# Two more ff tiles computed the plain way ahead of the pairs that use sums of blocks

## The chip, the cores and the metric

The kernel runs on one core of a Trainium2 chip. Five engines of the core work side by side, each through its own list of instructions in a fixed order: PE (matrix products), DVE and ACT (elementwise work), POOL (little here) and SP (issues the loads and stores). An instruction that needs another engine's result waits for it, and all that stands behind it in the same list waits too. The metric is the device time of one execution in microseconds (us).

## What is computed

Two layers of an encoder for T = 576 tokens of width 1024 (512 tokens of new streams and 64 of running ones). Each layer is a SwGLU block, a mixer with three groups of heads, and a second SwGLU block, every one between norms:

```python
D_MODEL = 1024; D_FF = 2816; DEPTH = 2

def _swiglu(x, w_gate, w_up, w_down):
    return (jax.nn.silu(x @ w_gate) * (x @ w_up)) @ w_down

# layer l
x = x + 0.5 * post1(swiglu_1(pre1(x)))
x = x + post2(mixer(pre2(x)))
x = x + 0.5 * post3(swiglu_2(pre3(x)))
```

So there are four SwGLU stages in a run. In each, gate and up are products of a 1024 x 2816 matrix with the 576 tokens.

## The kernel before

**Tiling.** The tokens lie along the free dimension, in two halves of 288 columns (`HALF`). The 1024 rows of x are 8 k tiles of 128, the 2816 columns of a weight are 22 ff tiles of 128. Every product is made of three matmuls (`three`, through `mul`, L68), since each operand is split into a high part and a rest: high x high, high x low, low x high. The names are `wh`, `wl` for a weight, `hh`, `hl` for x, `th`, `tl` for sums of blocks of x. A split is one copy on ACT (L126 or L138) and one subtraction on DVE (L127 or L139).

**The plain way.** `unit` takes one 128-column chunk of a weight, and for 8 k tiles and 2 halves issues 8 x 2 x 3 = 48 matmuls of 288 columns into two PSUM tiles named `u`. Gate and up of one ff tile need two chunks. `evac` then reads them half by half: DVE `g = u * rbc` (L339, gate times the norm's factor), ACT silu (L340), DVE `g = g * u` (L341, times up).

**The way with sums of blocks.** `seven` computes gate and up of two neighbouring ff tiles f and f+1 in one go: the weight is cut into 2 x 2 blocks (k tiles 0 to 3 and 4 to 7, ff tiles f and f+1), the tokens into two halves, and seven block products replace eight, at the price of sums: of weight blocks (DVE L478, L480, L488, L497, 128x1024 each) and of blocks of x (`combine`). Each product is 24 matmuls, a pair 7 x 24 = 168. In the plain way the same two ff tiles take four chunks, 4 x 48 = 192. The products of a pair stand in the order X (x block as it is), Q (t1), X (t2), Q (x block), X (t3), R (x block), X (t4). Q with t1 needs the first sum of x blocks in both of its k groups; R needs the sums of weights' splits that come last.

**A stage** (`ffn`, L327). (1) ff tiles 0 and 1 were loaded ahead as four chunks; `units` computes them for the first half of the tokens, then for the second, as x becomes ready behind the norm. (2) `combine` makes t1 to t4 for two k groups: for each, 8 scaled copies of x blocks on ACT (L427, `b<-x,colg`), four sums on DVE (L436, L438, L440, L442), and four splits into `th` (ACT L138, L141) and `tl` (DVE L139, L142). It ends with the stores of x to DRAM. (3) `evac` of the second half of ff tiles 0 and 1. (4) `for f in range(2, NF, 2)`: ten pairs in `seven`. (5) the down projection.

**Order and buffers.** The order on each engine is set when the program is built, by a list scheduler that takes the code's order and the tiles' dependencies. Raw weights have 6 buffers (`wr`, also the weight sums `ws`), their split parts 7 each (`wh`, `wl`), and matmul results 6 PSUM banks (`mm`), handed out in turn: the seventh `u`, `X`, `Q` or `R` tile can only be begun when the reader of the first is done.

Of the kernel before, what the change touches and what calls it, by code (L numbers as in the profile page):

```python
# [15 lines left out]
P = 128  # L16
# [8 lines left out]
NF = D_FF // P  # L25
# [24 lines left out]
class Net:  # L50
# [276 lines left out]
    def ffn(self, l, j, gpost, gpre, gain, nxt, packed):  # L327
        nc = self.nc
        wg, wu, wd = self.i["ffn_w_gate"][l, j], self.i["ffn_w_up"][l, j], self.i["ffn_w_down"][l, j]
        r, r2, rbc = self.rn, self.rn2, self.rbc  # L330
        g = {}


        def evac(f, hf, pg, pu):
            c0, n = HALF[hf]
            if hf == 0:
                g[f] = self.slot("g")
            t = g[f][:, c0:c0 + n]
            nc.vector.tensor_tensor(t, pg[:, :n], rbc[:, c0:c0 + n], op=ALU.mult)  # L339
            nc.scalar.activation(t, t, AF.Silu)  # L340
            nc.vector.tensor_tensor(t, t, pu[:, :n], op=ALU.mult)  # L341

        chs, self.ahead = self.ahead, None
        for hf in (0, 1):
            o = self.units(chs, hf, 2 if gpost is self.g0 else 4)
            if hf == 0:
                self.until(lambda: 0 in self.stats_done)
                for f in (0, 1):
                    evac(f, 0, o[2 * f][0], o[2 * f + 1][0])
        chs = None  # L350
        ops = self.combine(gain)
        self.until(lambda: 1 in self.stats_done)
        for f in (0, 1):
            evac(f, 1, o[2 * f][1], o[2 * f + 1][1])
        o = None
        for f in range(2, NF, 2):
            self.seven(f, wg, wu, ops, g, rbc)
        ops.clear()
        self.h = {}

        d = []
        for a, (g0, g1) in enumerate(GROUPS):
            first, last = a == 0, a == len(GROUPS) - 1
            gh, gl = {}, {}
            for f in range(g0, g1):
                gh[f], gl[f] = self.slot("gh", F32R), self.slot("gl", F32R)
                self.split(gh[f], gl[f], g.pop(f))
            if last:
                acc = self.slot("acc2")
                self.recall()  # L370
                if gpre is None:
                    self.spawn(self.rows_of_x(), 25.0)

            def run(m, ch, hfs):
                ps = {hf: self.mm("d") for hf in hfs}
                for f in range(g0, g1):
                    for hf in hfs:
                        c0, n = HALF[hf]
                        self.three(ps[hf][:, :n], ch[0][:, f - g0], ch[1][:, f - g0],
                                   gh[f][:, c0:c0 + n], gl[f][:, c0:c0 + n], f == g0, f == g1 - 1)  # L380
                    self.tick()
                for hf in hfs:
                    c0, n = HALF[hf]
                    sl = slice(c0, c0 + n)
                    if first:
                        if hf == 0:
                            d.append(self.slot("d"))
                        nc.scalar.activation(d[m][:, sl], ps[hf][:, :n], AF.Copy)
                        continue
                    nc.vector.tensor_tensor(d[m][:, sl], d[m][:, sl], ps[hf][:, :n], op=ALU.add)  # L390
                    if last:
                        self.square_sum(acc, d[m], sl, m)
                        if gpre is None:
                            nc.scalar.activation(d[m][:, sl], d[m][:, sl], AF.Copy, scale=gpost[m])

            tail = KT - 3 if last else KT
            for m in range(tail):
                run(m, self.cols(wd, m * P, P, g0, g1 - g0), (0, 1))
            if last:
                chs = [self.cols(wd, m * P, P, g0, g1 - g0) for m in range(tail, KT)]  # L400
                self.ahead = [self.cols(*q) for q in nxt]
                for hf in (0, 1):
                    for m in range(tail, KT):
                        run(m, chs[m - tail], [hf])
                    self.after(hf, d, acc, gpost, gpre, (r, r2), packed)
# [1051 lines left out]
```

## Time and profile before

| what | value |
|---|---|
| device time, median of 3 runs (lowest, highest) | 2313.14 us (2313.03, 2313.42) |
| the profiled execution's own time | 2313.43 us |
| span of its trace, first to last instruction | 2311.6 us |
| mean granted clock of PE | 0.979 of 2.4 GHz |
| busy PE, DVE, ACT, POOL | 96%, 69%, 48%, 10% |
| share of the chain that ended last: PE, DVE, ACT | 76%, 14%, 4% |
| the first pair of `seven` in the four SwGLU stages | 30.16, 33.20, 31.21, 33.12 us |
| a later pair | 22.40 us |

The page's first part gives busy time by engine. Windows of the trace give busy time and the granted clock of a stretch. "Idle before" is time in which an engine stood still just before an instruction, and behind it stands what ended that. PE's matmuls overlap, so their pace is read from one start to the next and not from one's length. A pair is counted here from the first start of its product X to the first start of the next pair's.

### The profile page before, as it was taken

Reading aid. Unit: us, or ns where it says so; the run is one execution under the profiler, and the core shown is the slowest. Engines: PE = TensorE matmul, PEld = TensorE weight load, DVE = VectorE, ACT = ScalarE, POOL = GpSimd, SP = SyncE. Lnnn points to the kernel's source line nnn. Section 1 sums busy time; section 2 is a strip of 40 time slices with the busy share of each in tenths; the row PEclk is TensorE's granted clock in tenths of the full one; section 3 lists DMA queues with packets and bytes.
Section 4 is the critical chain, followed back from the end, with each engine's and each line's share of the span. In section 5 each row is a group of like instructions: output and inputs, shape, how many; then the busy total and the mean of one; then the engine's idle time right before and its main releaser. Section 6 shows DMA issues by size and latency. Waiting matters only on the chain.

```text
span 2311.6 us, 39493 instructions
## 1 busy us (share of the span) xinstructions
PE 2217.3 (96%) x15892; PEld 2155.0 (93%) x15892; DVE 1594.7 (69%) x2671; ACT 1114.0 (48%) x1945; POOL 225.4 (10%) x230
## 2 busy tenths in 40 slices
PE   8999999998899899999989999999988998999998
PEld 7999999888799799999979999998887998999998
DVE  6888643787567888744588885438875678877443
ACT  7444442465554644443355444325646546444423
POOL 0000000343301100000020000004332020000000
PEclk9999999999999899999999999999999999999999
DMA  6333442222122233344123334423121312333421
GB/s 195 103 101 92 119 133 83 92 57 77 60 59 65 90 101 96 88 128 132 47 86 101 93 90 122 132 74 101 39 86 48 96 60 83 93 92 103 118 77 42
DMA packets 339787, 211.06 MB, mean 91 GB/s; under 512 B 17634, under 2 KB 319956, under 8 KB 339604
## 3 DMA queue, kind: packets, MB, share of 16 engines
q1 hardware_dynamic: 339604, 208.54, 30.3%
q8 instruction: 125, 2.05, 0.4%
q14 instruction: 58, 0.48, 0.1%
HBM read 190.11 MB, written 18.38 MB: 90 GB/s over the span
## 4 chain that ended last, share of the span: by engine, by line
PE 76%; DVE 14%; ACT 4%; issue 3%; POOL 3%; DMA 0%; SPq 0%; POOLq 0%; DVEq 0%; ACTq 0%
PE d L68 23%; PE X L68 22%; PE Q L68 11%; PE R L68 6%; PE wo L68 4%; PE u L68 3%; DVE zb L706 2%; PE n L68 2%; DVE hl L142 2%; DVE x L256 1%; PE sc L68 1%; DVE d L253 1%; DVE wl L127 1%; DVE wl L139 1%; PE q L68 1%
## 5 line engine op out<-in xcount | busy, mean ns | idle before, releaser
L68 PE MATMUL d<-gh,wh 128*128 128x288 f32 x1408 | 413.5, 297 | 2.7 <-ACT gh L138 2.7
L68 PE MATMUL d<-gl,wh 128*128 128x288 f32 x1408 | 413.9, 295 | 0.0
L68 PE MATMUL d<-gh,wl 128*128 128x288 f32 x1408 | 412.7, 294 | 0.0
L127 DVE TENSOR_TENSOR wl<-wr,wh 128x1024 fp32r<-128x1024 f32 (+2 forms) x174 | 203.4, 1173 | 175.9 <-ACT wh L126 175.1
L126 ACT ACTIVATE wh<-wr 128x1024 fp32r<-128x1024 f32 (+2 forms) x174 | 174.8, 1008 | 287.3 <-PE d L68 163.9
L68 PE MATMUL X<-th,wh 128*128 128x288 f32 x960 | 286.8, 299 | 0.0
L68 PE MATMUL X<-tl,wh 128*128 128x288 f32 x960 | 285.5, 297 | 0.0
L68 PE MATMUL X<-th,wl 128*128 128x288 f32 x960 | 284.5, 296 | 0.0
L68 PEld LDWEIGHTS d<-gh,wh 128*128 128x128 f32 x1408 | 262.3, 187 | 3.6 <-ACT gh L138 3.6
L68 PEld LDWEIGHTS d<-gh,wl 128*128 128x128 f32 x1408 | 264.8, 188 | 0.0
L68 PEld LDWEIGHTS d<-gl,wh 128*128 128x128 f32 x1408 | 264.1, 188 | 0.0
L138 ACT ACTIVATE wh<-wr 128x1024 fp32r<-128x1024 f32 x160 | 168.4, 1055 | 148.0 <-PE R L68 68.5
L139 DVE TENSOR_TENSOR wl<-ws,wh 128x1024 fp32r<-128x1024 f32 x120 | 147.0, 1225 | 105.4 <-ACT wh L138 105.2
L139 DVE TENSOR_TENSOR wl<-wr,wh 128x1024 fp32r<-128x1024 f32 x160 | 194.7, 1222 | 8.2 <-ACT wh L138 6.8
L138 ACT ACTIVATE wh<-ws 128x1024 fp32r<-128x1024 f32 x120 | 127.3, 1060 | 150.4 <-DVE ws L497 97.8
L151 POOL TENSOR_TENSOR p<-m,mhalf 128x3 f32<-128x3 f32 (+1 forms) x14 | 14.4, 1028 | 1739.4 <-DVE m L234 1535.1
L68 PEld LDWEIGHTS X<-th,wl 128*128 128x128 f32 x960 | 183.1, 191 | 0.0
L68 PEld LDWEIGHTS X<-tl,wh 128*128 128x128 f32 x960 | 182.8, 190 | 0.0
L68 PEld LDWEIGHTS X<-th,wh 128*128 128x128 f32 x960 | 182.6, 190 | 0.0
L390 DVE TENSOR_TENSOR d<-d,d 128x288 f32<-128x288 f32 x128 | 55.2, 454 | 179.6 <-PE d L68 179.5
L68 PE MATMUL u<-hh,wh 128*128 128x288 f32 x480 | 148.3, 312 | 3.0 <-ACT x L1363 1.5
L68 PE MATMUL u<-hl,wh 128*128 128x288 f32 x480 | 148.0, 309 | 1.2 <-DVE hl L142 1.2
(364 smaller groups left out, 5857.6 us busy)
## 6 DMA issues: line engine op xcount, KB each, us to landing
wr<-ffn_w_gate SPq DMA_DIRECT2D x160, 256.0 KB, 3.0
wr<-ffn_w_up SPq DMA_DIRECT2D x160, 256.0 KB, 3.4
wr<-ffn_w_down SPq DMA_DIRECT2D x64, 512.0 KB, 4.2
wr<-w_in SPq DMA_DIRECT2D x30, 512.0 KB, 3.7
xd<-x SPq DMA_DIRECT2D x48, 288.0 KB, 2.1
x<-xd SPq DMA_DIRECT2D x48, 288.0 KB, 6.0
wr<-ffn_w_down SPq DMA_DIRECT2D x32, 384.0 KB, 3.6
wr<-w_out SPq DMA_DIRECT2D x16, 512.0 KB, 3.4
```

What stands on the lines that cost most here:

```text
L68: self.nc.tensor.matmul(out, lhsT, rhs, start=start, stop=stop, skip_group_check=onto)
L126: nc.scalar.activation(hi[:, :a * b], raw[:, :a * b], AF.Copy)
L127: nc.vector.tensor_tensor(lo[:, :a * b], raw[:, :a * b], hi[:, :a * b].bitcast(F32), op=ALU.subtract)
L138: nc.scalar.activation(hi, src, AF.Copy)
L139: nc.vector.tensor_tensor(lo, src, hi.bitcast(F32), op=ALU.subtract)
L142: nc.vector.scalar_tensor_tensor(lo, src, scale, hi.bitcast(F32), op0=ALU.mult, op1=ALU.subtract)
L151: self.nc.gpsimd.tensor_tensor(out, m, self.mhalf[:, :n], op=ALU.pow)
L253: nc.vector.scalar_tensor_tensor(d[s][:, sl], d[s][:, sl], gpost[s], bc, op0=ALU.mult, op1=ALU.mult)
L256: nc.vector.tensor_tensor(self.x[k][:, sl], self.x[k][:, sl], d[k][:, sl], op=ALU.add)
L390: nc.vector.tensor_tensor(d[m][:, sl], d[m][:, sl], ps[hf][:, :n], op=ALU.add)
L706: nc.vector.tensor_tensor(zo, qv[rs, :, h:], ev[rs, :, h:], op=ALU.mult)
```

## The change

ff tiles 2 and 3 are taken out of the loop over pairs. Their gate and up chunks go through `cols` and `unit`, as four plain chunks of 48 matmuls in the order gate 2, up 2, gate 3, up 3; behind each up stands `evac` for both halves. The loop over pairs begins at f = 4, so there are nine pairs in a stage in place of ten. `combine` stays where it was, ahead of both.

```diff
         for f in (0, 1):
             evac(f, 1, o[2 * f][1], o[2 * f + 1][1])
         o = None
-        for f in range(2, NF, 2):
+        for f in (2, 3):
+            pg = self.unit(self.cols(wg, f * P))
+            pu = self.unit(self.cols(wu, f * P))
+            for hf in (0, 1):
+                evac(f, hf, pg[hf], pu[hf])
+        for f in range(4, NF, 2):
             self.seven(f, wg, wu, ops, g, rbc)
```

The order on the engines in the second of the four stages (layer 0, second SwGLU). In all stages PE's order differs in this place alone, but for some matmuls of ff tiles 0 and 1 that change places in the first stage.

PE, where ff tiles 0 and 1 end. Before; `bc` is the norm's factor spread over the partitions:

```order
L68 MATMUL u_8304<-hl_8277,wh_7820 128x288
L68 MATMUL u_8304<-hh_8276,wl_7821 128x288
L73 MATMUL bc_8481<-ident_c,rn_7928 128x128 x3
L68 MATMUL X_8515<-hh_7977,wh_8501 128x288
L68 MATMUL X_8515<-hl_7978,wh_8501 128x288
L68 MATMUL X_8515<-hh_7977,wl_8502 128x288
L68 MATMUL X_8515<-hh_7977,wh_8501 128x288
```

PE in the same place now:

```order
L68 MATMUL u_8298<-hl_8271,wh_7814 128x288
L68 MATMUL u_8298<-hh_8270,wl_7815 128x288
L73 MATMUL bc_8475<-ident_c,rn_7922 128x128 x3
L68 MATMUL u_8492<-hh_7971,wh_8488 128x288
L68 MATMUL u_8492<-hl_7972,wh_8488 128x288
L68 MATMUL u_8492<-hh_7971,wl_8489 128x288
L68 MATMUL u_8493<-hh_8152,wh_8488 128x288
```

The 168 matmuls of the first pair (X, Q, X, Q, X, R, X) are gone from here, and 192 plain ones stand in their place; `u_8492` and `u_8493` are the two halves of gate 2.

DVE, where `combine` ends (its last `tl`). Before, with the weight splits of the first pair among its rows:

```order
L440 TENSOR_TENSOR b_8450<-b_8450,b_8444 128x576
L442 TENSOR_TENSOR b_8447<-b_8441,b_8447 128x576
L139 TENSOR_TENSOR wl_8611<-wr_8495,wh_8610 128x1024
L139 TENSOR_TENSOR tl_8465<-b_8450,th_8464 128x576
L139 TENSOR_TENSOR wl_8642<-wr_8512,wh_8641 128x1024
L139 TENSOR_TENSOR tl_8470<-b_8447,th_8469 128x576
L139 TENSOR_TENSOR wl_8674<-wr_8498,wh_8673 128x1024
```

DVE in the same place now (the lines behind L357 have moved by 5, so L440 reads L445 here):

```order
L445 TENSOR_TENSOR b_8444<-b_8444,b_8438 128x576
L447 TENSOR_TENSOR b_8441<-b_8435,b_8441 128x576
L502 TENSOR_TENSOR ws_8737<-ws_8737,wr_8744 128x1024
L139 TENSOR_TENSOR tl_8459<-b_8444,th_8458 128x576
L139 TENSOR_TENSOR tl_8464<-b_8441,th_8463 128x576
L339 TENSOR_TENSOR g_8598<-u_8492,rbc_7921 128x288
L339 TENSOR_TENSOR g_8598<-u_8493,rbc_7921 128x288
```

The two reads of gate 2's banks (L339) stand behind the whole of `combine` and behind three weight sums of the first pair that is left (f = 4).

ACT, behind the norm's factor of the first half (`rbc`). Before:

```order
L215 ACTIVATE rbc_7927<-bc_8288 128x288
L427 ACTIVATE b_8409<-x_7696,colg 128x288
L340 ACT_TABLE_LOAD
L340 ACTIVATE g_8293<-g_8293 128x288
L340 ACTIVATE g_8297<-g_8297 128x288
L427 ACTIVATE b_8409<-x_7697,colg 128x288
```

ACT in the same place now:

```order
L215 ACTIVATE rbc_7921<-bc_8282 128x288
L126 ACTIVATE wh_8663<-wr_8661 128x1024
L340 ACT_TABLE_LOAD
L340 ACTIVATE g_8287<-g_8287 128x288
L340 ACTIVATE g_8291<-g_8291 128x288
L432 ACTIVATE b_8403<-x_7690,colg 128x288
```

The split of up 3's weight (`wh_8663`) has come in ahead of the table load, the silu and the copies for `combine`. It takes the eighth `wh` where there are seven buffers, and so waits for PE to be done with the first chunk of ff tile 0.

## Rows read from the trace of the kernel before

**Rows 1.** The page: busy time, and the chain that ended last.

```profile
PE 2217.3 (96%) x15892; PEld 2155.0 (93%) x15892; DVE 1594.7 (69%) x2671; ACT 1114.0 (48%) x1945; POOL 225.4 (10%) x230
PE 76%; DVE 14%; ACT 4%; issue 3%; POOL 3%; DMA 0%; SPq 0%; POOLq 0%; DVEq 0%; ACTq 0%
```

**Rows 2.** Windows: the four first pairs, then a later one.

```profile
core 0: us, PE busy (x) PEld busy (x) DVE busy (x) ACT busy (x) POOL busy (x), PEclk, DMA share, GB/s
46.75:76.91 30.16, 24.71 (x171) 23.78 (x169) 28.07 (x36) 19.82 (x32) 0.00 (x0) 0.94 0.30 86
773.77:806.97 33.20, 26.69 (x172) 25.29 (x169) 31.46 (x41) 21.53 (x35) 0.00 (x0) 0.85 0.28 80
1188.86:1220.07 31.21, 25.05 (x172) 24.12 (x170) 28.50 (x37) 20.55 (x34) 0.00 (x0) 0.95 0.29 85
1917.42:1950.54 33.12, 26.61 (x172) 25.33 (x170) 31.46 (x41) 21.54 (x35) 0.00 (x0) 0.90 0.28 79
76.91:99.31 22.40, 22.40 (x171) 22.40 (x169) 19.83 (x26) 10.79 (x15) 0.00 (x0) 1.00 0.34 97
```

**Rows 3.** PE's waits over the run: total us, times, longest us.

```profile
PE R L68 <- DVE wl L139: 12.8, 4, 3.5
PE Q L68 <- ACT th L138: 7.1, 4, 2.6
PE R L68 <- ACT wh L138: 3.3, 4, 1.4
PE Q L68 <- DVE tl L139: 1.4, 4, 0.4
```

**Rows 4.** Chain in the second stage's first pair: start, us, what.

```profile
778.65 0.37 DVE g L339
...
787.94 0.67 DVE tl L139
788.61 1.15 DVE wl L139
...
789.80 0.61 PE R L68
```

**Rows 5.** Windows, columns as in rows 2: two inside first pairs, one ahead.

```profile
783.20:793.44 10.24, 6.82 (x28) 6.12 (x27) 10.24 (x12) 6.67 (x12) 0.00 (x0) 0.50 0.37 108
59.57:62.98 3.41, 2.91 (x12) 2.92 (x13) 3.41 (x5) 0.41 (x2) 0.00 (x0) 0.50 0.50 142
1179.20:1182.50 3.30, 3.30 (x16) 3.30 (x16) 2.85 (x6) 2.89 (x7) 1.77 (x1) 0.50 0.07 18
```

**Rows 6.** PE's timeline: plain matmuls of the third stage, then a first pair.

```profile
1183.18 0.29 PE L68 MATMUL u<-hl,wh 128*128 128x288 f32 x1
...
1188.49 0.29 PE L68 MATMUL u<-hh,wl 128*128 128x288 f32 x1
...
790.20 0.44 PE L68 MATMUL X<-th,wh 128*128 128x288 f32 x1
790.44 0.44 PE L68 MATMUL X<-tl,wh 128*128 128x288 f32 x1
```

**Rows 7.** DVE's timeline, second stage: two evacuations, and the end of `combine`.

```profile
774.49 0.46 DVE L339 TENSOR_TENSOR g<-u,rbc 128x288 f32<-128x288 f32 x1 [3.34 <-ACT rbc L215]
...
782.54 0.45 DVE L341 TENSOR_TENSOR g<-g,u 128x288 f32<-128x288 f32 x1
...
789.65 0.76 DVE L139 TENSOR_TENSOR tl<-b,th 128x576 fp32r<-128x576 f32 x1
```

**Rows 8.** ACT's timeline, second stage, around the table load.

```profile
762.74 1.28 ACT L340 ACT_TABLE_LOAD   x1
...
764.72 3.08 ACT L427 ACTIVATE b<-x,colg 128x288 f32<-128x288 f32 x7
...
774.05 0.41 ACT L215 ACTIVATE rbc<-bc 128x288 f32<-128x288 f32 x1 [3.53 <-PE bc L73]
```

**Rows 9.** DMA issues on SP, loads of 512 KB: median us to landing.

```profile
wr<-ffn_w_down SPq DMA_DIRECT2D x64, 512.0 KB, 4.2
```

## The prediction

> **What bounds the kernel now.** I read the page first: PE is busy 96% of the span and holds 76% of the chain that ended last, DVE 14% [rows 1]. So a change pays if it takes matmuls away, or if it takes away time in which PE stands or runs at a lower clock. This one adds matmuls, and so the question is what it takes from PE's idle time. I then looked at windows by stage. A pair of `seven` takes 22.40 us at full clock, with PE busy throughout [rows 2]: 168 matmuls, 0.1333 us each. But the first pair of each of the four SwGLU stages takes 30.16, 33.20, 31.21 and 33.12 us, at a granted clock of 0.94, 0.85, 0.95 and 0.90 [rows 2]. Together that is 127.69 us where four later pairs take 89.60: an excess of 38.1 us.
>
> PE's waits say what most of it is. R waits 12.8 us for `wl` and 3.3 for `wh`, Q waits 7.1 us for `th` and 1.4 for `tl`, each four times in the run [rows 3]; these sixteen waits lie in the four first pairs, one of each kind in each, and come to 24.6 us. What they wait for is shown by the chain: in the second stage's first pair it runs through DVE, in the rest of `combine` and the weight splits that stand between its rows, up to PE's R at 789.80 us [rows 4]. Here DVE is the engine that sets the end: 31.46 us busy of 33.20 [rows 2]. The other 38.1 - 24.6 = 13.5 us is clock: inside the first pairs there are stretches with a granted clock of 0.50 (1.2 of 2.4 GHz), behind the waits: 10.24 us long in the second stage, 3.41 in the first [rows 5]. There matmuls start 0.24 us apart [rows 6] in place of 0.133.
>
> **What the change removes.** The first pair, with its waits and its lower clock: -127.69 us. Of the pair's work beside PE, four weight sums on DVE, and seven weight splits on ACT and DVE with it, are gone from the place where DVE sets the end.
>
> **What it adds on PE.** 4 chunks of 8 x 2 x 3 = 48 plain matmuls, 192 a stage. Their pace is on the trace: 41 plain matmuls in the third stage start between 1183.18 and 1188.49 us, 40 steps of 0.1328 us [rows 6], the pair's pace within reading. I take the pair's 0.1333: 192 x 0.1333 = 25.6 us a stage, 102.4 us in four. So with PE never waiting: 102.4 - 127.69 = **-25.3 us**. Against a pair without waits a stage pays 3.2 us for its 24 more matmuls (24 x 0.1333), so the change pays if over 3.2 of a stage's 9.5 us of excess go.
>
> The Trainium skill, TensorE: Matmul & The Clock Gate, section Back-to-back issue gap, gives N / 2.4 + 2.5 ns for a warm matmul by itself, 122.5 ns at 288 columns; the trace's 133 ns disagrees, and decides. By the page's figure four stages would come to an estimated 94.1 us and the change to -33.6; the sum above doesn't use it.
>
> **Do the waits go, or move?** The plain chunks need x and their weights only, not `combine`. PE begins gate 2 where X began (T = 773.77 us in the second stage [rows 2]), and the first pair that is left begins 25.6 us later, at 799.4. The last of `combine` ended at 789.65 + 0.76 = 790.4 us before [rows 7], 9 us ahead of that. What can still hold PE is its banks: six in turn, two to a chunk. Each release against its need in the second stage:
> - up 2 (T + 6.4 = 780.2 us) takes the banks of ff tile 0's second half, last read ahead of ff tile 1's L339, which stood at 778.65 [rows 4].
> - gate 3 (T + 12.8 = 786.6) takes those of ff tile 1's second half, last read by L341 at 782.54 + 0.45 = 783.0 [rows 7]: 3.6 us to spare, and less by what `combine` comes later (below).
> - up 3 (T + 19.2 = 793.0) takes gate 2's own, read by two L339 that stand behind all of `combine`. This is the tightest place, and it hangs on ACT.
>
> **ACT and DVE, second and fourth stage.** The split of up 3's weight now stands ahead of the table load, the silu and the copies for `combine`. It waits for a `wh` buffer until ff tile 0's first chunk is done; 48 of the plain matmuls come after that, so about 773.7 - 6.4 = 767.3 us. Behind it: its own 1 us (as a long row, 1.1), the load 1.28, two silu, eight copies (seven take 3.08 [rows 8], so 3.5): they end near 773.4, where they ended at 764.72 + 3.08 = 767.8. Of these 5.6 us DVE stood idle for 3.34 anyway, waiting for the second half's `rbc` [rows 7, 8]. From 773.4 on DVE has, by the order, 6 long rows (1024 columns), 16 of 576 and 4 of 288 ahead of the first L339 of gate 2. From start to start these take 1.14, 0.67 and 0.37 us [rows 4]: 6.84 + 10.72 + 1.48 = 19.0 us. So that L339 starts at 792.4 and ends at 792.9 us, level with the 793.0 at which it is needed. I take a wait of nought here, and keep 1 us a stage for the range: the count leaves no room. In the first and third stage no split stands ahead of the copies, and L339 is there some us early.
>
> **SP.** Four loads of 512 KB take the place of eight of 256 KB, with the same bytes. One of 512 KB lands 4.2 us from its issue [rows 9], and the chunks are needed 6.4 us apart. Nothing, hidden behind the chunk before; without that cover 4.2 us for one chunk.
>
> **Sum.** The profiled execution took 2313.43 us, of which the trace spans 2311.6, and the rest stays. 2313.43 - 25.3 = 2288.1; the median lies 0.3 us below it: **2288.0 us** forecast, 1.1% less.
>
> **Rivals.**
> *The clock stays low* (0.06). The 13.5 us might not hang on these waits. For it: the clock is 0.50 in other stretches as well, in 1179.20 to 1182.50 us with PE busy throughout [rows 5]. Against: inside later pairs it is 1.00 [rows 2], and the four first pairs differ only by their waits. It gives 2288.0 + 13.5 = 2301.5. The Trainium skill, TensorE: Matmul & The Clock Gate, section "A second HAM failure mode: psum-queue depth-cycling", has a form of it: short idle times between groups of matmuls, from banks that are turned over, make the clock go up and down. Rows 5 agree that the clock falls behind short waits; that bank turnover alone makes such waits here, no run shows.
>
> *ACT's delay gets through* (0.09). If DVE loses 3 us more in the two stages with the moved split, as by standing still once more for `th` the way it did for `rbc` (3.34 us [rows 7]), up 3 waits 3 us there, and a stretch of 3.41 us at half clock may follow [rows 5], worth 1.7: 2 x 4.7 = 9.4, so 2297.4. For it: the count above has no room; against: in that count ACT has its `th` ready while DVE is in a long row.
>
> *PE waits for DVE as long as now* (0.04), the other sign. The queue on DVE, not the place of the pair, would set the end: it is the bound, 31.46 of 33.20 us [rows 2], and the change takes nothing from `combine`. If up 3 must wait for it as Q and R do, 24.6 us of waits and 13.5 of clock stay, and the 96 more matmuls (12.8 us) come on top: 2313.1 + 12.8 = 2325.9. It decides from the point at which a stage loses (25.3 + 4.6) / 4 = 7.5 us in waits and clock, with the first L339 some 6 us behind T + 19.2. Against: 25.6 us of PE work lie now between the start of the queue and its end, where the first wait was 6.4 us behind X.
>
> That the change does not what it says: the order of the changed program shows the 192 matmuls where they should be, so under 0.01.
>
> **How the numbers follow.** Forecast 0.80, its own range 2285.5 to 2293: downwards the plain pace of 0.1328 (0.4 us) and one stretch at half clock less elsewhere (1.7 us), upwards 1 us of waiting and half of such a stretch in each of two stages, and 1 us for the rest. The first two rivals lie above it. To hold 8 in 10 the range goes up into ACT's delay: 2285.5 to 2297.5. What a measurement can tell here from no change is about 0.2%, 4.6 us. Faster by more: forecast and the first two rivals, with a little taken off, 0.94; within 0.2%: 0.02; slower by more: 0.04.
>
> **What would show it.** In the profile after: no PE waits of Q and R for `th`, `tl`, `wh`, `wl` in rows like 3; the time from the last of ff tile 1 to the first X 25.6 us in each stage, at a granted clock of 1.00; the first pair left 22.40 us. Wrong would be: `u` waiting for DVE L339 over 1 us in a stage, an X later than T + 26, or the clock at 0.50 within it.

## The result, and the profile after

The changed kernel took 2285.9 us (median; 2283.0 to 2288.3) against 2313.1 us before: a ratio of 0.9884, 95% interval 0.9867 to 0.9901, so 27.2 us or 1.2% faster. The forecast was 2288.0. The profiled execution took 2284.6 us, with a span of 2282.8.

The windows of the trace after, from each stage's T (where the first plain chunk begins) to the first X, and two pairs behind it. Columns: window, its length, busy time of PE, PEld, DVE, ACT, POOL, granted clock, DMA share, GB/s.

```profile
46.61:72.18 25.57, 25.57 (x194) 25.57 (x194) 23.40 (x31) 12.91 (x22) 0.00 (x0) 1.00 0.30 86
764.85:790.43 25.58, 25.58 (x196) 25.58 (x194) 25.09 (x35) 16.59 (x29) 0.00 (x0) 1.00 0.18 52
1170.55:1196.12 25.57, 25.57 (x195) 25.57 (x193) 23.93 (x33) 15.28 (x28) 0.00 (x0) 1.00 0.29 83
1896.24:1921.81 25.57, 25.57 (x195) 25.57 (x194) 23.21 (x33) 15.30 (x27) 0.00 (x0) 1.00 0.22 63
72.18:94.58 22.40, 22.40 (x171) 22.40 (x169) 15.69 (x21) 10.21 (x14) 0.00 (x0) 1.00 0.25 73
790.43:812.82 22.39, 22.39 (x171) 22.39 (x169) 15.55 (x21) 10.17 (x14) 0.00 (x0) 1.00 0.29 84
```

These stand where the first four lines of [rows 2] stood. The 30.16, 33.20, 31.21 and 33.12 us have become 25.57 or 25.58 in every stage, PE is busy from end to end, and the clock is 1.00. The first pair that is left takes 22.40 us like any other. In the second stage DVE is busy 25.09 us of 25.58: the work that held PE is still there, beside PE now.

The chain that ended last, second stage (start, us, what), shows the same; where DVE stood in [rows 4] there is only PE:

```profile
764.77 0.33 PE bc L73 x3
765.10 25.49 PE u L68 x192
790.59 3.19 PE X L68 x24
```

None of the four kinds of waits of [rows 3] is left in PE's waits over the run; what PE's rows of `u` still wait for (waiter, line, what for: total us, times, longest) lies outside the four stretches above, and Q, R and X have no row:

```profile
PE u L68 <- ACT x L1368: 1.5, 2, 0.9
PE u L68 <- DVE on L839: 1.4, 2, 0.7
PE u L68 <- DVE hl L142: 1.2, 4, 0.4
```

The place that the prediction called the tightest, in DVE's and ACT's timelines of the second stage (start, us, engine, line, operation):

```profile
758.03 1.06 ACT L126 ACTIVATE wh<-wr 128x1024 fp32r<-128x1024 f32 x1 [3.11 <-PE u L68]
759.11 1.28 ACT L340 ACT_TABLE_LOAD   x1
761.09 3.51 ACT L432 ACTIVATE b<-x,colg 128x288 f32<-128x288 f32 x8
...
762.93 0.76 DVE L441 TENSOR_TENSOR b<-b,b 128x576 f32<-128x576 f32 x1
763.60 1.22 DVE L485 TENSOR_TENSOR wr<-wr,wr 128x1024 f32<-128x1024 f32 x1
765.21 0.76 DVE L139 TENSOR_TENSOR tl<-b,th 128x576 fp32r<-128x576 f32 x1 [0.39 <-ACT th L138]
...
781.16 1.43 DVE L139 TENSOR_TENSOR tl<-b,th 128x576 fp32r<-128x576 f32 x2
782.50 0.83 DVE L339 TENSOR_TENSOR g<-u,rbc 128x288 f32<-128x288 f32 x2
```

The split of up 3's weight waits 3.11 us for PE and starts 6.8 us ahead of T = 764.85 (6.4 were counted); the copies end at 764.6, 0.25 ahead of T (0.4). The first L339 of gate 2 starts at T + 17.65 and is done about T + 18.1; up 3 needs it at T + 19.2. So there were 1.1 us of room where the prediction counted 0.1. In the first, third and fourth stage it starts at T + 13.4, 16.6 and 16.6, with 5.4, 2.1 and 2.2 us of room.

### The profile page after: what moved, and what is told of

It reads as the page before. It is cut to its first block, busy times and chain, and to the rows that moved or that the text cites. A ratio compares the mean times of both kernels' runs of the same rounds, so it can differ in the third digit from the quotient of the medians.

```text
span 2282.8 us, 39582 instructions
## 1 busy us (share of the span) xinstructions
PE 2214.3 (97%) x15988; PEld 2157.1 (94%) x15988; DVE 1554.9 (68%) x2627; ACT 1093.4 (48%) x1917; POOL 225.6 (10%) x230
## 4 chain that ended last, share of the span: by engine, by line
PE 80%; DVE 10%; ACT 3%; issue 3%; POOL 3%; DMA 0%; SPq 0%; POOLq 0%; DVEq 0%; ACTq 0%
PE d L68 24%; PE X L68 20%; PE Q L68 10%; PE u L68 8%; PE R L68 5%; PE wo L68 4%; DVE zb L711 2%; PE n L68 2%; PE sc L68 1%; DVE x L256 1%; DVE hl L142 1%; DVE d L253 1%; DVE wl L127 1%; PE q L68 1%; PE oT L68 1%
## 5 line engine op out<-in xcount | busy, mean ns | idle before, releaser
L127 DVE TENSOR_TENSOR wl<-wr,wh 128x1024 fp32r<-128x1024 f32 (+3 forms) x190 | 224.0, 1183 | 177.7 <-ACT wh L126 176.2
L126 ACT ACTIVATE wh<-wr 128x1024 fp32r<-128x1024 f32 (+3 forms) x190 | 191.5, 1011 | 297.2 <-PE d L68 166.9
L68 PE MATMUL X<-th,wh 128*128 128x288 f32 x864 | 255.7, 296 | 0.0
L68 PE MATMUL X<-tl,wh 128*128 128x288 f32 x864 | 254.9, 295 | 0.0
L68 PE MATMUL X<-th,wl 128*128 128x288 f32 x864 | 254.0, 294 | 0.0
L68 PE MATMUL u<-hh,wh 128*128 128x288 f32 x736 | 223.4, 305 | 3.1 <-ACT x L1368 1.5
L68 PE MATMUL u<-hl,wh 128*128 128x288 f32 x736 | 223.0, 303 | 1.2 <-DVE hl L142 1.2
L68 PE MATMUL u<-hh,wl 128*128 128x288 f32 x736 | 221.7, 302 | 0.0
L68 PEld LDWEIGHTS X<-th,wl 128*128 128x128 f32 x864 | 162.8, 188 | 0.0
L68 PEld LDWEIGHTS X<-tl,wh 128*128 128x128 f32 x864 | 162.2, 188 | 0.0
```

Source lines behind the costliest of these rows:

```text
L68: self.nc.tensor.matmul(out, lhsT, rhs, start=start, stop=stop, skip_group_check=onto)
L126: nc.scalar.activation(hi[:, :a * b], raw[:, :a * b], AF.Copy)
L127: nc.vector.tensor_tensor(lo[:, :a * b], raw[:, :a * b], hi[:, :a * b].bitcast(F32), op=ALU.subtract)
```

## Experiments

**What did Q and R wait for?** The kernel before with all ten pairs, and the work of `combine` left out:

```diff
         for q in range(2):
-            b = []
-            for kp in (q, q + 2):
-                for hf in range(2):
...
-            nc.vector.tensor_tensor(b21, b11, b21, op=ALU.subtract)
-            part("t4", b21)
+            ops["t1"].append(self.h[q, 0])
+            ops["t2"].append(self.h[q, 1])
+            ops["t3"].append(self.h[q + 2, 0])
+            ops["t4"].append(self.h[q + 2, 1])
```

> The kernel before, all ten pairs in seven, but t1 to t4 are given x blocks as they are: the copies, sums and splits of combine are left out, so gate and up come out as other numbers. Theory (Q and R of the first pair wait because combine stands in DVE's and ACT's queues around the pair's own sums and splits): all sixteen waits go, 24.6 us, and the 13.5 us of low clock with them; the first pairs take 22.4 us each, 2313.1 - 38.1 = 2275.0 us. Rival (the pair's own weight sums and splits are what R waits for, 16.1 us of the waits): Q's 8.5 us go, R's stay with most of the clock: 2300 to 2305 us.

Measured 2274.1 us, ratio 0.9837 (0.9823 to 0.9852). All four first pairs take 22.40 us; those of the second and third stage:

```profile
763.96:786.36 22.40, 22.40 (x171) 22.40 (x169) 19.40 (x26) 12.44 (x19) 0.00 (x0) 1.00 0.40 118
1167.17:1189.57 22.40, 22.40 (x171) 22.40 (x170) 20.64 (x27) 12.71 (x20) 0.00 (x0) 1.00 0.40 118
```

No wait and no low clock is left in them, R's included, although all weight sums and splits of the pair are still made. So `combine` was the cause of all sixteen waits, of R's through the queue: the weights' rows stood between and behind its rows. It also gives the floor for ten pairs, 2274: the changed kernel lies 12 us above it, about the price of its 96 more matmuls (12.8).

**Is it the place or the number of pairs?** The plain ff tiles behind the first pair (edit against the changed kernel):

```diff
-        for f in (2, 3):
+        self.seven(2, wg, wu, ops, g, rbc)
+        for f in (4, 5):
             pg = self.unit(self.cols(wg, f * P))
...
-        for f in range(4, NF, 2):
+        for f in range(6, NF, 2):
             self.seven(f, wg, wu, ops, g, rbc)
```

> The same two plain ff tiles, but behind the first pair: seven for 2 and 3, plain for 4 and 5, seven from 6. Theory (what counts is the place, as cover for combine): the first pairs keep their 30.2, 33.2, 31.2 and 33.1 us, and 96 more matmuls come on top: 2313.1 + 12.8 = 2325.9 us. Rival (nine pairs are better than ten wherever they stand, since a pair's sums and splits are gone from DVE and ACT): at or under 2313, down to 2288 us.

Measured 2324.1 us, ratio 1.0054 (1.0037 to 1.0071). In the second stage, the first pair and then the plain part:

```profile
774.86:808.05 33.19, 27.09 (x163) 25.69 (x162) 28.56 (x39) 20.79 (x35) 0.00 (x0) 0.79 0.39 111
808.05:833.65 25.60, 25.60 (x195) 25.60 (x194) 15.04 (x19) 6.88 (x10) 0.00 (x0) 1.00 0.21 61
```

The pair pays its 33.2 us as before, the plain part 25.60 on top; nine pairs are no gain by themselves. The same matmuls in another place are 38 us apart (2324.1 and 2285.9).

**Does more cover bring more?** Four plain ff tiles ahead, eight pairs (edit against the changed kernel):

```diff
-        for f in (2, 3):
+        for f in (2, 3, 4, 5):
             pg = self.unit(self.cols(wg, f * P))
...
-        for f in range(4, NF, 2):
+        for f in range(6, NF, 2):
```

> ff tiles 2 to 5 the plain way, ahead of eight pairs. Theory (one pair's worth of plain work covers all of combine, and no wait is left): 96 more matmuls and nothing for it, 2285.9 + 12.8 = 2298.7 us. Rival (cover is still short, as the count with no room for gate 2's L339 said): 2286 to 2292 us.

Measured 2300.5 us, ratio 0.9950 (0.9935 to 0.9965): 14.6 us above the changed kernel, where 12.8 were expected for the matmuls. Two plain ff tiles are cover enough; two more cost (2300.5 - 2285.9) / 4 = 3.7 us a stage. (The 1.8 us above the expected 12.8 are as much as a new wait of up 3 for L339 takes, 0.93 us in the second stage and again in the fourth.) Less cover than two ff tiles was not tried.

**Is the release of gate 2's banks what would hold PE next?** The changed kernel with DVE held up ahead of it (edit against the changed kernel):

```diff
-            nc.vector.tensor_tensor(b11, b11, b12, op=ALU.subtract)
+            for _ in range(1 + 7 * q):
+                nc.vector.tensor_tensor(b11, b11, b12, op=ALU.subtract)
             part("t1", b11)
```

> The changed kernel with seven more subtractions of 576 columns (0.67 us each) on DVE in combine, ahead of the second k group's t1; the sums are other numbers by that. By the order of the program five to six long rows of the pair f = 4 (1.14 us each) also move ahead of gate 2's L339, so it comes 10 to 11.5 us later. In the changed kernel this L339 has 5.4, 1.1, 2.1 and 2.2 us to spare in the four stages. Theory (PE is held by nothing but this release, and each us beyond the room is a us lost): up 3 waits about 6, 9, 8 and 8 us, 31 in all, and the clock falls behind the waits, 1.7 to 3.4 us a stage: 2286 + 31 + 7 to 14 = 2324 to 2331 us, slower than the kernel before. Rival (with 25.6 us of plain work PE is out of DVE's reach): 2286 to 2289 us.

Measured 2334.3 us, ratio 1.0094 (1.0079 to 1.0109): slower than the kernel before. That is above the 2324 to 2331 of its theory. PE's wait in the second stage, DVE's row that ends it, the stretch from T to the first X, and the part of it right behind the wait:

```profile
805.28 0.58 PE L68 MATMUL u<-hh,wh 128*128 128x288 f32 x1 [9.91 <-DVE g L339]
...
804.68 1.18 DVE L339 TENSOR_TENSOR g<-u,rbc 128x288 f32<-128x288 f32 x3
...
776.01:814.50 38.49, 28.58 (x195) 28.38 (x193) 30.29 (x43) 16.57 (x29) 0.00 (x0) 0.82 0.14 42
805.28:811.20 5.92, 5.92 (x25) 5.92 (x26) 1.67 (x5) 1.50 (x4) 0.00 (x0) 0.50 0.00 0
```

PE waited 7.0, 9.9, 10.1 and 9.9 us in the four stages, 36.9 where 31 were expected. In the second stage L339 came at T + 28.7, 11.0 us later than in the changed kernel; less the 1.1 of room that is the 9.9. In the other three it came about 12 us later, more than I had counted. The mechanism is the rival that was given 0.04, made to happen: in the second stage 38.49 - 25.58 = 12.9 us are lost, 9.9 by the wait and 3.0 behind it, where 25 matmuls run at a granted clock of 0.50. With 1.1 us of room in the second stage, two more long rows on DVE there (1.1 us each) would, as an estimate from this run, begin to cost time.

**Could the same be had without more matmuls?** Four kernels of ten pairs with other orders (edits against the kernel before). Copies first, then t1 of both k groups, t2, t3, t4:

```diff
+        bs = []
         for q in range(2):
...
-            b11, b12, b21, b22 = b
+            bs.append(b)
...
+        for b11, b12, b21, b22 in bs:
             nc.vector.tensor_tensor(b11, b11, b12, op=ALU.subtract)
             part("t1", b11)
+        for b11, b12, b21, b22 in bs:
             nc.vector.tensor_tensor(b11, b11, b22, op=ALU.add)
             part("t2", b11, -1.0)
...
```

> The kernel before with the rows of combine in another order: all sixteen copies first, then t1 of both k groups, then t2, t3, t4; ten pairs, no plain ff tiles added, the same work. Theory (in the first pair DVE is short of time as a whole, some 31 us of rows against 22.4 us of PE work): Q's waits for th and tl shrink, but what DVE does earlier for t1 it does later for the weights, and other products wait in its place: 2300 to 2311 us. Rival (the waits come from the order alone): Q's 8.5 us and its part of the clock go, and some of R's: 2290 to 2298 us.

The first pair's R put second:

```diff
         product(p1, "b11", X, True)
         p1 = None
+        if f == 2:
+            p2 = part(a12)
+            R = [self.mm("R"), self.mm("R")]
+            product(p2, "b21", R, True)
...
```

> The kernel before with the product R of each stage's first pair put second, behind the first X, so that 6.4 us of matmuls need no sum of x in place of 3.2; same work otherwise. Theory (DVE's total decides): R's 16.1 us of waits go to the products behind it, X with t2 and t4: 2303 to 2313 us. Rival (R waits only because its split stands late): 16.1 us and part of the clock go, 2290 to 2297 us.

Both of these:

> Both new orders together, copies first and R second, all sums on DVE. Theory (DVE's total decides): 2297 to 2308 us, still 10 us or more above the changed kernel's 2286. Rival (the order is all): both gains add up, 2275 to 2285 us, and plain ff tiles are not needed.

Both, and the four sums of the second k group on POOL:

```diff
+        nc.vector.tensor_tensor(bs[0][0], bs[0][0], bs[0][1], op=ALU.subtract)
+        part("t1", bs[0][0])
+        nc.gpsimd.tensor_tensor(bs[1][0], bs[1][0], bs[1][1], op=ALU.subtract)
+        part("t1", bs[1][0])
...
```

> As the kernel with both new orders, and the four sums of the second k group's x blocks on POOL in place of DVE: 4 x 0.67 us less on DVE in each stage, POOL having nothing else to do there (a sum of 128x576 took 1.61 us on it in the mixer). Ten pairs, no plain ff tiles added. Theory (time on DVE is what is short): this gets under what the order alone gives, waits of 1 to 3 us a stage and 1.7 us of low clock in each: 2275 + 4 to 12 + 0 to 7 = 2279 to 2294 us, at or under the changed kernel's 2286. Rival (POOL's slower sums only move the wait from DVE to POOL): at or above 2297 us.

| kernel | us | ratio to before (95%) |
|---|---|---|
| copies first | 2297.4 | 0.9939 (0.9925 to 0.9954) |
| R second | 2301.0 | 0.9957 (0.9945 to 0.9968) |
| both | 2297.8 | 0.9945 (0.9929 to 0.9960) |
| both, half the sums on POOL | 2292.6 | 0.9920 (0.9904 to 0.9937) |
| the changed kernel | 2285.9 | 0.9884 (0.9867 to 0.9901) |

PE's waits over the run in these four, in this order (the rows of Q, R and X over 0.5 us):

```profile
PE Q L68 <- DVE g L341: 12.4, 3, 4.1
PE X L68 <- ACT s L492: 2.4, 1, 2.4
...
PE X L68 <- ACT s L492: 10.4, 4, 2.8
PE X L68 <- DVE s L524: 5.5, 8, 0.8
PE Q L68 <- DVE tl L139: 1.1, 2, 0.6
PE Q L68 <- ACT th L138: 1.0, 2, 0.5
...
PE R L68 <- DVE g L341: 12.4, 3, 4.1
PE Q L68 <- DVE g L339: 4.3, 1, 4.3
...
PE Q L68 <- DVE g L339: 8.9, 3, 3.0
PE Q L68 <- DVE g L341: 4.9, 3, 3.1
PE X L68 <- DVE s L533: 1.4, 3, 0.7
```

Each new order takes most of the old waits away, and puts others in their place: with t1 early, the banks of ff tiles 0 and 1 are read later (L339, L341 stand behind the sums), and Q or R waits for those; with R early, X waits for ACT's copy of its banks. These waits come to 15 to 18 us a run, where they were 24.6. Copies first came out at the upper end of its rival's times, R second between theory and rival, both together at the lower end of its theory: order alone is worth 11 to 15 us, more than I gave it, but the two together are worth no more than one. With half the sums on POOL it is 5 us less, but not by less time on DVE: in the second stage the four rows taken off it are worth 2.7 us, and three of its own rows took 3.3 us longer while POOL was at its sums (last section). What the 5 us come from is not shown. The times of the fourth are in its theory's range, but not at or under the changed kernel's. None gets to the changed kernel: by the whole time, what a stage loses above the floor of 2274 is (2292.6 - 2274.1) / 4 = 4.6 us in the best of them, and (2285.9 - 2274.1) / 4 = 3.0 with the plain cover. Read from the traces, the second stage from T to its last matmul takes 366.99 us at the floor (763.96 to 1130.95), 372.15 in the best of the four orders (767.73 to 1139.88) and 370.09 in the changed kernel (764.85 to 1134.94): 5.2 and 3.1 us. Whether a finer order of DVE's rows would get below that stays open.

**Where do the 3 us beyond the first pairs come from?** In the first profiles the SwGLU stages account for 25.4 of 28.8 us of span; the mixers between them, with the same rows, took 742.6 us before and 739.4 after. Both kernels were profiled once more, unchanged:

> The changed kernel as it is, once more. In its first profile the four SwGLU stages were shorter by 25.4 us and the mixers between them, whose rows are the same in the same order, by 3.2 us. Theory (which rows of the mixer meet the stretches at half clock is chance): the plain chunks and pairs take the same 25.57 and 22.40 us to 0.1 us, the three stretches from the down projection to the next stage's T take others than 348.2, 35.6 and 355.6 us by up to 5, and their sum is 739 to 743; the median is 2285 to 2288 us, 25 to 27 under the kernel before. Rival (the change shortens the mixer too): the sum is 739.4 again within 0.5, and the median 28 to 29 us under.

> The kernel before as it is, once more, for the same question. Its three mixer stretches took 352.4, 37.4 and 352.8 us, 742.6 in all. Theory (chance): first pairs of 30.2, 33.2, 31.2 and 33.1 us again within 0.5, and a sum of the stretches between 739 and 743 that need not be 742.6. Rival (the mixer is slower in the kernel before): 742.6 again within 0.5.

Measured: 2285.1 us, ratio 0.9880 (0.9866 to 0.9895), for the changed kernel, and 2312.4, ratio 0.9997 (0.9988 to 1.0006), for the kernel before. The changed kernel is 28.2 us under the 2313.3 that it was compared with, where its theory said 25 to 27 and its rival 28 to 29; against 2312.4 it is 27.3. The three mixer stretches (end of the down projection to T), of the changed kernel again and then of the kernel before again:

```profile
416.50:766.55 350.05, 327.10 (x2175) 301.80 (x2174) 255.04 (x580) 195.07 (x406) 100.29 (x97) 0.97 0.26 78
1136.60:1172.14 35.54, 32.08 (x223) 31.09 (x221) 34.05 (x60) 19.67 (x44) 15.57 (x16) 0.90 0.28 97
1542.20:1899.84 357.64, 330.15 (x2175) 305.19 (x2174) 257.95 (x584) 194.94 (x406) 98.54 (x97) 0.96 0.25 75
...
422.09:772.43 350.34, 324.85 (x2175) 300.44 (x2175) 255.05 (x579) 193.28 (x404) 100.20 (x97) 0.98 0.24 73
1151.10:1188.52 37.42, 33.62 (x222) 32.64 (x221) 33.35 (x61) 18.52 (x43) 15.71 (x16) 0.86 0.22 78
1564.80:1915.90 351.10, 326.93 (x2176) 302.28 (x2174) 257.08 (x583) 193.19 (x404) 98.44 (x97) 0.97 0.24 72
```

743.2 us in all for the changed kernel and 738.9 for the one before: the other way round. So a sum of the mixers that is 3.2 us shorter is no property of the change, and that rival falls; both sums lie within 0.2 us of the theory's 739 to 743. The median nevertheless came out where the rival put it; the first pairs (below) can account for that. That the single stretches differ by chance alone is not shown: the second took 37.4 us in both executions of the kernel before and 35.6 and 35.5 in both of the changed one, the third 352.8 and 351.1 against 355.6 and 357.6. The second doesn't go with the plain chunks, though: it took 35.83 us with them behind the first pair (1156.81 to 1192.64) and 37.10 with four ff tiles ahead (1146.92 to 1184.02).

The first pairs of the kernel before are not fixed either:

```profile
47.38:77.73 30.35, 24.79 (x171) 23.86 (x169) 28.26 (x37) 19.84 (x32) 0.00 (x0) 0.94 0.29 86
772.43:806.63 34.20, 27.64 (x172) 26.28 (x170) 31.54 (x41) 21.51 (x35) 0.00 (x0) 0.85 0.27 77
1188.52:1220.28 31.76, 25.58 (x171) 24.65 (x170) 28.48 (x37) 20.54 (x34) 0.00 (x0) 0.89 0.29 83
1915.90:1950.09 34.19, 27.64 (x172) 26.28 (x170) 31.55 (x41) 21.52 (x35) 0.00 (x0) 0.85 0.27 77
```

130.50 us in place of 127.69 [rows 2], and I had expected each within 0.5 us: the second and fourth are 1.0 and 1.1 off, the third 0.55. Against four times 25.57 that is a gain of 28.2 us, beside 25.4 in the first profile. The waits in it are those of [rows 3], 24.5 us in place of 24.6, so the rest of the excess is what grew, from 13.5 to 16.4 us:

```profile
PE R L68 <- DVE wl L139: 13.7, 4, 3.5
PE Q L68 <- ACT th L138: 7.2, 4, 2.6
PE R L68 <- ACT wh L138: 2.4, 2, 1.4
...
PE Q L68 <- DVE tl L139: 1.2, 4, 0.4
```

## Why the prediction was right

- **The first pair's price.** The term of -127.69 us held for the execution it was read from; another gives 130.50. What is mis-sized is its clock part, 13.5 us of one execution: it was 16.4 in another. That can carry the gap between the 25.1 us forecast against the median and the 27.2 measured, though two profiles don't show that it does; the interval of the ratio, 22.9 to 30.8 us, holds both. The range had no term for it: downwards it had 2.1 us for other things, and the median lies 0.4 us above its lower end of 2285.5. The last step of the sum also slipped: 2288.1 less 0.3 is 2287.8.
- **The plain chunks.** 192 x 0.1333 = 25.6 us a stage; measured 25.57 or 25.58 in all four, 133 ns a matmul. That the estimate by the Trainium skill's figure (TensorE: Matmul & The Clock Gate, section Back-to-back issue gap; -33.6 us in all) was not used was right: by that formula a matmul of 288 columns would take an estimated 122.5 ns.
- **The waits.** All sixteen are gone; that they came from `combine` was shown by leaving it out, and that work which doesn't need it covers them by the place of that work: the same plain chunks behind the first pair leave them as they were.
- **The tight release.** Named rightly, but counted 1 us too late. The step that was off: I let DVE begin when the last of the eight copies ended. The first sum needs four of them, so L441 and L485 (1.8 us) ran at 762.93, beside the rest of the copies. The range had 1 us a stage for it; nothing was needed. The third stage, said to be some us early, had 2.1 us of room, hardly more than the second.
- **The clock.** The rival in which it stays low regardless of the waits fell: 1.00 in all four stretches after. The rule on banks that are turned over (the Trainium skill, TensorE: Matmul & The Clock Gate, section "A second HAM failure mode: psum-queue depth-cycling") did not come to bear: the four chunks turned the six banks over without a wait, at 1.00.
- **ACT's delay.** The copies ended 0.25 us ahead of T (6.0 ahead of it before, by [rows 2, 8]) where 0.4 was counted, but by two slips that cancel, which is luck. The terms named, with the two silu that take 0.7 us between the load and the copies in [rows 8], add up to 773.8 and not 773.4: by its own count the release would have come 0.3 us too late. And the split began 0.4 us sooner than T - 6.4; the three `bc` matmuls ahead of T, which the count left out, are some 0.25 of that. The delay was taken up by DVE's idle time and the overlap above.
- **Slower.** DVE's queue as the bound is real: with gate 2's L339 11 to 12 us later the change lost, 2334.3 us. One figure against this rival was misread: the first wait before begins 5.3 us behind X, not 6.4.

## What to carry to other kernels

When a preparation on one engine holds PE at the start of a stage, look for PE work of the same stage that doesn't need it, and compare its price (here 24 matmuls more, 3.2 us) with what the wait costs with its low clock (here 9.5 us). Check the next release in the buffers' rotation as closely as the wait that goes: it stood 1.1 us from being the new bound. Mere reorderings of the loaded engine's rows took the old waits away and made new ones, 15 to 18 us where they were 24.6.

## What was not expected of the hardware

PE's time in a stretch with waits was not the same in two executions of one kernel (33.20 and 34.20 us for the same pair, with a clock of 0.85 in both), while the stretches without waits repeat to 0.01 us (25.57 and 25.58 us in the four stages, in both executions of the changed kernel).

In the second stage of the last of the four orders, POOL's four sums of 128x576 took 1.64 to 1.91 us; its rows of this shape took 1.61 on average in the mixer of the kernel before. The three rows of this shape on DVE that lie beside POOL's last three took 1.63, 1.99 and 1.95 us, where the row before them took 0.75; they start 1.55, 1.91 and 1.87 us apart in place of 0.67. Those rows of POOL, then DVE's (start, us):

```profile
769.86 1.88 POOL L443 TENSOR_TENSOR b<-b,b 128x576 f32<-128x576 f32 x1 [3.14 <-DVE tl L139]
771.83 1.83 POOL L447 TENSOR_TENSOR b<-b,b 128x576 f32<-128x576 f32 x1
773.62 1.91 POOL L451 TENSOR_TENSOR b<-b,b 128x576 f32<-128x576 f32 x1
...
769.70 0.75 DVE L441 TENSOR_TENSOR b<-b,b 128x576 f32<-128x576 f32 x1
...
770.74 1.63 DVE L445 TENSOR_TENSOR b<-b,b 128x576 f32<-128x576 f32 x1
772.29 1.99 DVE L142 SCALAR_TENSOR_TENSOR tl<-b,th 128x576 fp32r<-128x576 f32 x1
774.20 1.95 DVE L449 TENSOR_TENSOR b<-b,b 128x576 f32<-128x576 f32 x1
```

So DVE's rows were slower beside POOL's sums here. The trace does not show what held them up, and no run separates it.
